# A mixer's attention weights for two of four head pairs turned by DMA transposes instead of TensorE, and its norms taken from row sums

## The chip, the cores and the metric

The kernel runs on one core of one Trainium2 chip. The core has a matrix engine (PE, with its own weight loads, PEld), a vector engine (DVE), a scalar engine (ACT), a further vector engine (POOL) and SP, which here issues DMAs. All engines run their own instruction streams in order and meet at semaphores. The metric is the device time of one execution in microseconds; lower is better.

## The reference

A decoder trunk of two layers over 256 tokens of width 1024. Each layer is a half FFN, a mixer and a second half FFN, each added to the scaled input and layer-normed:

```python
for l in range(DEPTH):                                          # 2
    h = _swiglu(x, ffn_w1[l, 0], ffn_w3[l, 0], ffn_w2[l, 0])    # 1024 -> 2816 -> 1024
    x = _layernorm(ALPHA * x + 0.5 * h, ln_g[l, 0], ln_b[l, 0])
    h = _mixer(x, l, ...)
    x = _layernorm(ALPHA * x + h, ln_g[l, 1], ln_b[l, 1])
    h = _swiglu(x, ffn_w1[l, 1], ffn_w3[l, 1], ffn_w2[l, 1])
    x = _layernorm(ALPHA * x + 0.5 * h, ln_g[l, 2], ln_b[l, 2])
```

The mixer projects x to u, v, q, k, val and two gates. Branch A is a gated unit with causal 128x128 position mixing. Branch B, which the change touches, is differential attention with 8 heads, each of two 64-wide query/key halves and a 128-wide value:

```python
p = jax.nn.softmax(where(mask, s, neg))     # s: b h m q k, m = 0, 1
a = p[:, :, 0] - lam * p[:, :, 1]           # the attention weights
o = einsum('bhqk,bkhe->bqhe', a, val)       # then a norm per head
```

The two branches, each times its gate, are summed and projected (w_out). Inputs and output are float32.

## The kernel before

**Tiles.** The 256 tokens are two tiles (t = 0, 1) of 128. Weights come from HBM in 1 MB chunks: `stream` issues one DMA on SP into `raw`, ACT copies each half to `whi` (line 174) and DVE subtracts to get the rest, `wlo` (line 178). A float32 product is three matmuls, hi·hi, lo·hi and hi·lo. `gemm_a2` does it with the weights as the stationary side: 16 matmuls `x,whi` 512 wide (line 283), then 16 `x,wlo` 256 wide (line 290), after which ACT takes one part of the bank out (`r`, line 291) and DVE adds the other (`gz` in the gates, line 293).

**Order.** PE runs in the order in which the program is written. The other engines' streams are ordered by a scheduler from priorities; `behind(x)` puts an instruction after x in that order, and `soon()` raises its priority. Side work is written as generators: `beside(task, d)` starts one after d beats of the main matmuls and `yield n` lets n beats pass, so that its PE instructions are put between the main ones. A beat is 0.65 for 8 matmuls of line 283 and 0.35 for 8 of line 290.

**A mixer.** The val gemm comes first, then eight `rope` gemms for q and k, two for each of four pairs of heads (hp = 0 to 3), then the gate gemms and the rest of branch A. `attend(hp)` runs as a side task: the scores of t=1 and then of t=0 on PE (line 837, into side banks), the masked maximum on DVE (845), Exp on ACT (847), `less` on DVE (856), which forms the weights a as `pp` tiles (128 queries by keys: 128x512 for t=1, 128x256 for t=0, two heads each). PE then turns them by six 128x128 transposes against an identity (871 and 876), ACT takes the two banks out to `aT` (873, 878), and PE multiplies them with val (884, 886). After that ACT copies the result out (`on`, 889) and squares it in its bank for the per-head norm (894, four times); POOL works out the reciprocal root; ACT scales (905), splits the halves of each float into two 16-bit planes (184), a DMA transpose on SP turns these (189), ACT joins the planes (195), and ACT and DVE form the operand `hb` (915, 916). So pair 2's work after its scores and pair 3's scores lie in the last q/k gemm and the first gate gemms; pair 3's transposes and value matmuls lie in the gate gemms.

**Banks and buffers.** PSUM has four main banks for the gemms and four side banks. Four 128x512 `pp` tiles belong to a pair's two score tiles (two halves each); `less` writes its result over one of the two and leaves the other unused.

**Norms.** After an FFN, `part_s` adds the product to x on DVE with the row sum as a by-product, and `finish_s` gets the mean from the sums, the variance from a Square on ACT with its own accumulation, and 1/sqrt by three steps on DVE. After a mixer, `part` adds and `bn_stats` (571) takes the statistics, `bn_aggr` (578) joins them, then the same three steps and the scaling (582). In both, the upper half of the normed tile goes out as 16-bit planes to a DMA transpose (`send`), the lower half is turned by PE (641), and ACT scales and splits both (646, 233, with DVE's 234) into the operand of the next FFN, whose first gemm starts with the parts of it that are there.

Of the kernel before, what the change touches and what calls it, by code (L numbers as in the profile page):

```python
# [15 lines left out]
U16 = mybir.dt.uint16  # L16
# [4 lines left out]
P = 128  # L21
# [37 lines left out]
def trunk(ctx, tc, x, xT, w13a, w13b, w2s, w2p, wb, wqk, wa, wbr, wo, gateb, sgug, sgub, sguwT, sgubias, lam, diffg,  # L59
# [25 lines left out]
    def side_bank():  # L85
        return psum.tile([P, 512], F32, tag="side", name=name("sbank"))
# [54 lines left out]
    def beside(task, delay):  # L141
        tasks.append([clock[0] + delay, task])
# [366 lines left out]
    class Norm:  # L509
# [29 lines left out]
            else:  # L539
                V.scalar_tensor_tensor(out=y, in0=y, scalar=scale, in1=v, op0=ALU.mult, op1=op)  # L540

        def part_s(self, t, c, ps):
            y = self.y[t][:, c * 512 : (c + 1) * 512]
            V.scalar_tensor_tensor(out=y, in0=y, scalar=1.0, in1=ps, op0=ALU.mult, op1=ALU.add,
                                   accum_out=self.st[t][:, c : c + 1])

        def finish_s(self, t, waits):
            y, st = self.y[t], self.st[t]
# [26 lines left out]
        def finish(self, t, waits):  # L575
            y = self.y[t]
            mv = sm("mv", 2)
            V.bn_aggr(out=mv, in_=self.st[t])
            if not self.last:
                r = rsqrt(mv[:, 1:2], self.eps)  # L580
                for s in (slice(512, D), slice(0, 512)):
                    self.ends[t] = V.tensor_scalar(out=y[:, s], in0=y[:, s], scalar1=mv[:, 0:1], scalar2=r,
                                                   op0=ALU.subtract, op1=ALU.mult).ins
                    if s.start:
                        self.send(t)
                beside(self.turned(t, waits), 0)
                return
            cuts = [slice(*c) for c in ((768, D), (0, 512), (512, 768))]
            ve, sd, r, a = (sm(n, 1) for n in ("ve", "nwy", "nwa", "nwy"))
            G.tensor_scalar(out=ve, in0=mv[:, 1:2], scalar1=self.eps, scalar2=None, op0=ALU.add)  # L590
            A.activation(sd, mv[:, 1:2], AF.Sqrt, bias=self.eps_t)
            rows = [y[:, s] for s in cuts]
            if t == NT - 1:
                rows[1:] = [side_bank()[:, : s.stop - s.start] for s in cuts[1:]]
                for b, s in zip(rows[1:], cuts[1:]):
                    PE.matmul(b, ident, y[:, s], start=True, stop=False)
                diag = self.minus[:, P : 2 * P]
                A.activation(diag, self.minus[:, :P], AF.Copy, scale=mv[:, 0:1])
                for b, s in zip(rows[1:], cuts[1:]):
                    PE.matmul(b, diag, self.g[:, s], start=False, stop=True)  # L600
            for s in cuts[: 1 if t == NT - 1 else 3]:
                V.scalar_tensor_tensor(out=y[:, s], in0=y[:, s], scalar=mv[:, 0:1], in1=self.g[:, s],
                                       op0=ALU.subtract, op1=ALU.mult)
            V.reciprocal(out=r, in_=sd)
            V.tensor_scalar(out=a, in0=r, scalar1=r, scalar2=ve, op0=ALU.mult, op1=ALU.mult)
            V.tensor_scalar(out=r, in0=a, scalar1=3.0, scalar2=r, op0=ALU.subtract, op1=ALU.mult)
            for n, (s, v) in enumerate(zip(cuts, rows)):
                V.scalar_tensor_tensor(out=y[:, s], in0=v, scalar=r, in1=self.b[:, s], op0=ALU.mult, op1=ALU.add)
                (nc.sync, A)[n % 2].dma_start(out[t * P : (t + 1) * P, s], y[:, s])
# [178 lines left out]
    def mixer(l, i, norm):  # L788
# [34 lines left out]
        def attend(hp, qT, kT):  # L823
# [27 lines left out]
            def less(t, pp):  # L851

                nk = (t + 1) * P
                for j in range(2):
                    s = slice(j * nk, (j + 1) * nk)
                    V.scalar_tensor_tensor(out=pp[0][:, s], in0=pp[1][:, s], scalar=c4[:, t * 2 + j : t * 2 + j + 1],
                                            in1=pp[0][:, s], op0=ALU.mult, op1=ALU.add)
                return pp[0]
# [3 lines left out]
            first = exps(0)  # L862
            V.reciprocal(out=rc, in_=sums[:, 4:])
            V.scalar_tensor_tensor(out=c4, in0=rc, scalar=neg_lam[l], in1=sums[:, :4], op0=ALU.mult, op1=ALU.mult)
            second, first = less(1, second), less(0, first)
            yield 2.6
            b = side_bank()
            for j in range(2):
                for c in range(2):
                    o = (j * 2 + c) * P  # L870
                    PE.transpose(b[:, o : o + P], second[:, o : o + P], ident)
            aT1 = slots("aT", 2)[0]
            A.activation(aT1, b, AF.Copy)
            b = side_bank()
            for j in range(2):
                PE.transpose(b[:, j * P : (j + 1) * P], first[:, j * P : (j + 1) * P], ident)
            aT0 = slots("aT", 2)[0][:, :T]
            A.activation(aT0, b[:, :T], AF.Copy)
            yield 2.3
            b = side_bank()  # L880
            for j in range(2):
                h = hp * 2 + j
# [120 lines left out]

        def done(t, ps):
            for h in range(2):
                ln.part(t, h * 512, ps[h])
            ln.finish(t, ((2, 1.5), (2, 1))[t])

        gemm_b2([wo[l, 0], wo[l, 1]], view(m_hi), view(m_lo), done)
        return ln.close()  # L1010
# [98 lines left out]
```

## Time and profile before

| | us |
|---|---|
| median of 3 runs | 1212.89 (1212.53 to 1213.18) |
| the profiled execution | 1213.48 |
| its span, first to last instruction | 1211.8 |
| PE busy | 1203.9 (99%) |
| DVE busy | 947.9 (78%) |
| ACT busy | 852.3 (70%) |
| POOL busy | 90.3 (7%) |

The span is what the profile's rows divide up; the 1.7 us between it and the execution's own time lies outside them. "Busy" is the time that at least one instruction of an engine was in flight. The granted clock of the matrix engine was 1.000 over the span. A row of the timeline gives the start, the duration, the engine, the line, the operation with its operands and the count of instructions that it joins; brackets hold the idle time before it and what ended that. Durations of rows that follow each other on DVE and ACT overlap by some 0.06 to 0.1 us, so steps are best read from start to start.

### The profile page before, as it was taken

To read this page: it belongs to the slowest core of one execution; us is meant where nothing else is said; L and a number is where in the kernel's file an instruction comes from. 1 tells how busy PE (TensorE), PEld (TensorE's weight loads), DVE (VectorE), ACT (ScalarE), POOL (GpSimd) and SP (SyncE) were. 2 spreads that over 40 slices of the span, in tenths; PEclk is the share of its full clock that TensorE was granted. 3 is DMA by queue.
4 is the path that set the end of the run, shared out by engine and by line. 5 is a ranking of instruction groups with operands and counts; after the bars stand their busy time and mean duration, and the time that the engine had idled before them with its cause. 6 is when DMAs were issued, how large, how long until landed. Compare 5 with 4: busy or idle time off the path is not lost.

```text
span 1211.8 us, 16532 instructions
## 1 busy us (share of the span) xinstructions
PE 1203.9 (99%) x5961; PEld 1011.5 (83%) x5961; DVE 947.9 (78%) x1540; ACT 852.3 (70%) x1376; POOL 90.3 (7%) x184
## 2 busy tenths in 40 slices
PE   9999999999999999999999999999999999999998
PEld 8888888888888878888888888888888888888886
DVE  6658998885696976579985679989756878847797
ACT  6677677679865585776776776776898555767761
POOL 0100000233300000000000000003331000000000
PEclk9999999999999999999999999999999999999999
DMA  8985665655764658666668665766648556676551
GB/s 321 317 267 174 212 249 204 231 178 164 229 227 168 217 180 280 191 187 218 232 210 274 194 179 209 252 226 197 211 143 273 176 174 217 203 257 210 184 204 46
DMA packets 101346, 257.00 MB, mean 212 GB/s; under 512 B 66528, under 2 KB 67600, under 8 KB 74640
## 3 DMA queue, kind: packets, MB, share of 16 engines
q1 hardware_dynamic: 97296, 243.03, 59.9%
q0 software_dynamic: 3536, 12.13, 3.2%
q8 instruction: 46, 0.75, 0.3%
q10 hardware_dynamic: 432, 0.79, 0.2%
q14 instruction: 36, 0.29, 0.1%
HBM read 235.47 MB, written 1.05 MB: 195 GB/s over the span
## 4 chain that ended last, share of the span: by engine, by line
PE 93%; DVE 5%; ACT 1%; issue 1%; DVEq 0%; ACTq 0%
PE bank L271 35%; PE sbank L271 24%; PE bank L283 17%; PE bank L290 9%; PE sbank L283 2%; PE bank L446 2%; PE sbank L290 1%; PE sbank L837 1%; PE sbank L969 1%; PE sbank L886 1%; DVE wlo L178 1%; DVE nwa L248 1%; DVE nwy L249 0%; DVE x L234 0%; DVE st L571 0%
## 5 line engine op out<-in xcount | busy, mean ns | idle before, releaser
L178 DVE TENSOR_TENSOR wlo<-raw,whi 128x1024 fp32r<-128x1024 f32 (+1 forms) x396 | 436.2, 1124 | 144.2 <-ACT whi L174 113.5
L174 ACT ACTIVATE whi<-raw 128x1024 fp32r<-128x1024 f32 (+1 forms) x396 | 372.9, 971 | 123.8 <-PE bank L283 40.1
L271 PE MATMUL bank<-whi,x 128*128 128x512 f32 x840 | 263.3, 390 | 0.0
L271 PEld LDWEIGHTS bank<-whi,x 128*128 128x128 f32 x840 | 157.7, 188 | 32.9
L271 PE MATMUL bank<-wlo,x 128*128 128x512 f32 x420 | 163.5, 389 | 0.0
L271 PE MATMUL sbank<-whi,x 128*128 128x512 f32 x512 | 158.9, 389 | 0.0
L283 PE MATMUL bank<-x,whi 128*128 128x512 f32 x640 | 156.0, 394 | 0.0
L283 PEld LDWEIGHTS bank<-x,whi 128*128 128x128 f32 x640 | 117.1, 188 | 26.4 <-issue 2.3
L271 PEld LDWEIGHTS sbank<-whi,x 128*128 128x128 f32 x512 | 96.1, 188 | 20.0
L353 ACT ACTIVATE shi<-raw 128x1024 fp32r<-128x1024 f32 (+1 forms) x80 | 73.4, 947 | 51.8 <-DVE raw L368 26.4
L271 PE MATMUL sbank<-wlo,x 128*128 128x512 f32 x256 | 99.6, 389 | 0.0
L355 DVE TENSOR_TENSOR slo<-raw,shi 128x1024 fp32r<-128x1024 f32 (+1 forms) x80 | 85.3, 1087 | 14.1 <-ACT shi L353 13.2
L271 PEld LDWEIGHTS bank<-wlo,x 128*128 128x128 f32 x420 | 78.9, 188 | 16.1
L290 PE MATMUL bank<-x,wlo 128*128 128x256 f32 x640 | 85.9, 285 | 0.0
L290 PEld LDWEIGHTS bank<-x,wlo 128*128 128x128 f32 x640 | 81.6, 191 | 2.2
L291 ACT ACTIVATE r<-bank 128x256 f32<-128x256 f32 x112 | 41.4, 376 | 24.0 <-PE bank L290 24.0
L271 PEld LDWEIGHTS sbank<-wlo,x 128*128 128x128 f32 x256 | 48.0, 188 | 9.9
L271 PE MATMUL sbank<-whi,hhi 128*128 128x512 f32 x144 | 56.3, 391 | 0.0
L271 PE MATMUL sbank<-whi,hlo 128*128 128x512 f32 x144 | 56.1, 389 | 0.0
L271 PE MATMUL sbank<-wlo,hhi 128*128 128x512 f32 x144 | 56.0, 389 | 0.0
L506 POOL DMA_DIRECT2D bc<-in_lng x6 | 3.2, 529 | 696.0 <-DVE bc L505 696.0
L710 ACT ACTIVATE planes<-silu 128x1024 uint16<-128x1024 uint16 x40 | 42.0, 1053 | 7.3 <-DVE silu L709 6.2
(249 smaller groups left out, 1997.7 us busy)
## 6 DMA issues: line engine op xcount, KB each, us to landing
raw<-in_w13b SPq DMA_DIRECT2D x76, 1024.0 KB, 5.3
raw<-in_w2p SPq DMA_DIRECT2D x24, 1024.0 KB, 4.9
raw<-in_wa SPq DMA_DIRECT2D x24, 1024.0 KB, 5.3
raw<-in_w2s SPq DMA_DIRECT2D x20, 1024.0 KB, 4.9
raw<-in_wb SPq DMA_DIRECT2D x16, 1024.0 KB, 5.1
raw<-in_wqk SPq DMA_DIRECT2D x16, 1024.0 KB, 4.9
raw<-in_wbr SPq DMA_DIRECT2D x16, 1024.0 KB, 4.8
raw<-in_w13a SPq DMA_DIRECT2D x8, 1024.0 KB, 4.8
```

The costliest lines, as they stand in the source:

```text
L174: copied = A.activation(h, r, AF.Copy)
L178: V.tensor_tensor(out=w, in0=r, in1=h.bitcast(F32), op=ALU.subtract)
L248: V.tensor_scalar(out=a, in0=y, scalar1=y, scalar2=ve, op0=ALU.mult, op1=ALU.mult)
L271: PE.matmul(ps, xx, w, start=start and n == 0, stop=stop and n == 2)
L283: PE.matmul(b[-1], hi[:, k * P : (k + 1) * P], xc(k), start=k == 0, stop=False)
L290: PE.matmul(b[n][:, :T], lo[:, k * P : (k + 1) * P], xc(k)[:, :T], start=False, stop=k == KT - 1)
L291: emptied[0] = A.activation(r[:, s], b[n][:, T:], AF.Copy, scale=scale).ins
L353: A.activation(h, r, AF.Copy)
L355: V.tensor_tensor(out=w, in0=r, in1=h.bitcast(F32), op=ALU.subtract)
L446: PE.matmul(ps[t][m], x[:, j, o + t * P : o + (t + 1) * P], y, start=k0 + j == 0 and o == 0 and y is hi, stop=k0 + j == KT - 1 and y is lo)
L710: A.activation(pk.rearrange("p (w k) -> p w k", w=2), s.bitcast(U16).rearrange("p (k w) -> p w k", w=2), AF.Copy)
L837: PE.matmul(banks[m][:, j * nk : (j + 1) * nk], rows(qT, m, j, t * P, P), rows(kT, m, j, 0, nk), start=True, stop=True)
```

## The change

1. In pairs 2 and 3 of each mixer, the six PE transposes and two ACT copies out of PSUM are replaced. DVE copies each weight tile into two 16-bit planes (new line 879), in the `pp` tile that `less` left unused; two DMA transposes on SP (8 and 4 blocks of 128x128 16-bit numbers) turn the planes; three beats later DVE joins the planes to `aT` and half a tile (new line 885), placed behind the latest add of a gemm's bank. The value matmuls follow two beats after that, where before they followed the transposes by 2.3.
2. The mixers' norms use `part_s` and `finish_s`. `bn_stats` and `bn_aggr` go, a Square on ACT comes; `part_s` gets the scale and the same `behind` that `part` had. Only the last norm still uses `finish`.

In a whole run that is 24 PE transposes, 8 ACT copies, 8 `bn_stats` and 4 `bn_aggr` fewer, and 16 DVE copies, 8 DMA transposes and 4 Squares with their small instructions more. The order of PE is otherwise the same, and POOL's too. Lines after the edit carry numbers shifted by -8 ahead of the new lines (837 is now 829) and by +8 behind them (894 is now 902).

```diff
--- before.py
+++ after.py
@@ -539,10 +539,11 @@
             else:
                 V.scalar_tensor_tensor(out=y, in0=y, scalar=scale, in1=v, op0=ALU.mult, op1=op)
 
-        def part_s(self, t, c, ps):
+        def part_s(self, t, c, ps, scale=1.0):
             y = self.y[t][:, c * 512 : (c + 1) * 512]
-            V.scalar_tensor_tensor(out=y, in0=y, scalar=1.0, in1=ps, op0=ALU.mult, op1=ALU.add,
-                                   accum_out=self.st[t][:, c : c + 1])
+            with behind(self.xlo.get((0, 0))):
+                V.scalar_tensor_tensor(out=y, in0=y, scalar=scale, in1=ps, op0=ALU.mult, op1=ALU.add,
+                                       accum_out=self.st[t][:, c : c + 1])
 
         def finish_s(self, t, waits):
             y, st = self.y[t], self.st[t]
@@ -576,15 +577,6 @@
             y = self.y[t]
             mv = sm("mv", 2)
             V.bn_aggr(out=mv, in_=self.st[t])
-            if not self.last:
-                r = rsqrt(mv[:, 1:2], self.eps)
-                for s in (slice(512, D), slice(0, 512)):
-                    self.ends[t] = V.tensor_scalar(out=y[:, s], in0=y[:, s], scalar1=mv[:, 0:1], scalar2=r,
-                                                   op0=ALU.subtract, op1=ALU.mult).ins
-                    if s.start:
-                        self.send(t)
-                beside(self.turned(t, waits), 0)
-                return
             cuts = [slice(*c) for c in ((768, D), (0, 512), (512, 768))]
             ve, sd, r, a = (sm(n, 1) for n in ("ve", "nwy", "nwa", "nwy"))
             G.tensor_scalar(out=ve, in0=mv[:, 1:2], scalar1=self.eps, scalar2=None, op0=ALU.add)
@@ -862,21 +854,37 @@
             first = exps(0)
             V.reciprocal(out=rc, in_=sums[:, 4:])
             V.scalar_tensor_tensor(out=c4, in0=rc, scalar=neg_lam[l], in1=sums[:, :4], op0=ALU.mult, op1=ALU.mult)
+            free2, free1 = second[1], first[1]
             second, first = less(1, second), less(0, first)
-            yield 2.6
-            b = side_bank()
-            for j in range(2):
-                for c in range(2):
-                    o = (j * 2 + c) * P
-                    PE.transpose(b[:, o : o + P], second[:, o : o + P], ident)
-            aT1 = slots("aT", 2)[0]
-            A.activation(aT1, b, AF.Copy)
-            b = side_bank()
-            for j in range(2):
-                PE.transpose(b[:, j * P : (j + 1) * P], first[:, j * P : (j + 1) * P], ident)
-            aT0 = slots("aT", 2)[0][:, :T]
-            A.activation(aT0, b[:, :T], AF.Copy)
-            yield 2.3
+            if hp < HEADS // 4:
+                yield 2.6
+                b = side_bank()
+                for j in range(2):
+                    for c in range(2):
+                        o = (j * 2 + c) * P
+                        PE.transpose(b[:, o : o + P], second[:, o : o + P], ident)
+                aT1 = slots("aT", 2)[0]
+                A.activation(aT1, b, AF.Copy)
+                b = side_bank()
+                for j in range(2):
+                    PE.transpose(b[:, j * P : (j + 1) * P], first[:, j * P : (j + 1) * P], ident)
+                aT0 = slots("aT", 2)[0][:, :T]
+                A.activation(aT0, b[:, :T], AF.Copy)
+                yield 2.3
+            else:
+                half = slots("half", 2)[0]
+                tts = []
+                for (p, spare), dst in (((second, free2), slots("tt", 2)[0]), ((first, free1), half[:, :T])):
+                    pk = spare.bitcast(U16)
+                    V.tensor_copy(pk.rearrange("p (w k) -> p w k", w=2), p.bitcast(U16).rearrange("p (k w) -> p w k", w=2))
+                    tts.append(turning(pk, pk.shape[1] // (2 * P), dst))
+                yield 3
+                aT1, aT0 = slots("aT", 2)[0], half[:, T:]
+                for dst, tt in zip((aT1, aT0), tts):
+                    with behind(added[0]):
+                        V.tensor_copy(dst.bitcast(U16).rearrange("p (k w) -> p k w", w=2),
+                                      tt.rearrange("p (w k) -> p k w", w=2))
+                yield 2
             b = side_bank()
             for j in range(2):
                 h = hp * 2 + j
@@ -1003,8 +1011,8 @@
 
         def done(t, ps):
             for h in range(2):
-                ln.part(t, h * 512, ps[h])
-            ln.finish(t, ((2, 1.5), (2, 1))[t])
+                ln.part_s(t, h, ps[h], ln.scale)
+            ln.finish_s(t, ((2, 1.5), (2, 1))[t])
 
         gemm_b2([wo[l, 0], wo[l, 1]], view(m_hi), view(m_lo), done)
         return ln.close()
```

Three places show what moves on DVE and ACT. All are in the mixer of layer 0.

First DVE, between `less` of pair 2 (856) and the scores of pair 3: `qk` is pair 3's k operand, `gz` the first gate tiles. Before:

```order
L856 SCALAR_TENSOR_TENSOR pp_2583<-pp_2588,c_2528,pp_2583 128x128 x2
L817 TENSOR_TENSOR qk_2547<-qk_2547,swap_2546 128x512
L178 TENSOR_TENSOR wlo_2966<-raw_2959,whi_2965 128x1024
L293 TENSOR_TENSOR gz_2610<-bank_2568,r_2609 128x256
L293 TENSOR_TENSOR gz_2610<-bank_2599,r_2609 128x256
L178 TENSOR_TENSOR wlo_3038<-raw_3035,whi_3037 128x1024
L178 TENSOR_TENSOR wlo_3042<-raw_3035,whi_3041 128x1024
L293 TENSOR_TENSOR gz_2698<-bank_2667,r_2697 128x256
L293 TENSOR_TENSOR gz_2698<-bank_2676,r_2697 128x256
```

and with the change:

```order
L879 COPY pp_2541<-pp_2536 128x1024
L879 COPY pp_2588<-pp_2583 128x512
L809 TENSOR_TENSOR qk_2547<-qk_2547,swap_2546 128x512
L178 TENSOR_TENSOR wlo_2960<-raw_2953,whi_2959 128x1024
L293 TENSOR_TENSOR gz_2616<-bank_2568,r_2615 128x256
L293 TENSOR_TENSOR gz_2616<-bank_2605,r_2615 128x256
L178 TENSOR_TENSOR wlo_3032<-raw_3029,whi_3031 128x1024
L178 TENSOR_TENSOR wlo_3036<-raw_3029,whi_3035 128x1024
L293 TENSOR_TENSOR gz_2692<-bank_2673,r_2691 128x256
L885 COPY aT_2726<-tt_2600 128x1024
L885 COPY half_2599<-half_2599 128x512
L293 TENSOR_TENSOR gz_2692<-bank_2682,r_2691 128x256
```

The two plane copies stand ahead of the `qk` add on which the next scores depend, and the two joins ahead of the second add of the second `gz`.

Second ACT, from pair 1's `on` (889, with the four squares of its bank) to the second gate tile. Before:

```order
L889 ACTIVATE on_2636<-sbank_2629 128x512
L894 ACTIVATE sbank_2629,ss_2638<-sbank_2629 128x128
L174 ACTIVATE whi_3037<-raw_3035 128x1024
L894 ACTIVATE sbank_2629,ss_2638<-sbank_2629 128x128
L932 ACTIVATE gate_2554<-gz_2610,gbh 128x256
L894 ACTIVATE sbank_2629,ss_2638<-sbank_2629 128x128
L932 ACTIVATE gate_2554<-gz_2610,gbh 128x256
L894 ACTIVATE sbank_2629,ss_2638<-sbank_2629 128x128
L873 ACTIVATE aT_2690<-sbank_2685 128x512
L878 ACTIVATE aT_2695<-sbank_2692 128x256
L174 ACTIVATE whi_3041<-raw_3035 128x1024
L291 ACTIVATE r_2697<-bank_2667 128x256
```

and with the change:

```order
L174 ACTIVATE whi_3031<-raw_3029 128x1024
L897 ACTIVATE on_2642<-sbank_2635 128x512
L940 ACTIVATE gate_2554<-gz_2616,gbh 128x256
L902 ACTIVATE sbank_2635,ss_2644<-sbank_2635 128x128
L940 ACTIVATE gate_2554<-gz_2616,gbh 128x256
L902 ACTIVATE sbank_2635,ss_2644<-sbank_2635 128x128
L174 ACTIVATE whi_3035<-raw_3029 128x1024
L902 ACTIVATE sbank_2635,ss_2644<-sbank_2635 128x128
L291 ACTIVATE r_2691<-bank_2673 128x256
L902 ACTIVATE sbank_2635,ss_2644<-sbank_2635 128x128
L291 ACTIVATE r_2691<-bank_2682 128x256
L940 ACTIVATE gate_2555<-gz_2692,gbh 128x256 x2
```

The two `aT` copies are gone; the last two squares of line 894 (now 902) stand behind a weight copy and a bank's `r` copy.

Third DVE again, at the joins of pair 3; `turned` and `hb` are pair 0's. Before:

```order
L916 SCALAR_TENSOR_TENSOR hb_1906<-turned_2881,dgs,hb_1906 128x256
L916 SCALAR_TENSOR_TENSOR hb_1907<-turned_2881,dgs,hb_1907 128x256
L293 TENSOR_TENSOR gz_2909<-bank_2872,r_2908 128x256
L293 TENSOR_TENSOR gz_2909<-bank_2887,r_2908 128x256
L178 TENSOR_TENSOR wlo_3179<-raw_3176,whi_3178 128x1024
```

and with the change:

```order
L293 TENSOR_TENSOR gz_2818<-bank_2808,r_2817 128x256
L924 SCALAR_TENSOR_TENSOR hb_1906<-turned_2884,dgs,hb_1906 128x256
L924 SCALAR_TENSOR_TENSOR hb_1907<-turned_2884,dgs,hb_1907 128x256
L293 TENSOR_TENSOR gz_2900<-bank_2875,r_2899 128x256
L885 COPY aT_2934<-tt_2803 128x1024
L885 COPY half_2802<-half_2802 128x512
L293 TENSOR_TENSOR gz_2900<-bank_2890,r_2899 128x256
```

The two joins stand behind the two `hb` rows and the first `gz` add.

## The prediction

> **What bounds the kernel now.** I read the page first: busy times, then the chain that ended last.
>
> ```profile
> PE 1203.9 (99%) x5961; PEld 1011.5 (83%) x5961; DVE 947.9 (78%) x1540; ACT 852.3 (70%) x1376; POOL 90.3 (7%) x184
> PE 93%; DVE 5%; ACT 1%; issue 1%; DVEq 0%; ACTq 0%
> ```
>
> PE has work in flight 99% of the span, and the chain runs over PE for 93% of it. So an edit pays only by what it takes out of PE's stream, and costs only where it makes PE wait. The view of PE's waits says how little it waits today: its largest items beyond the start and the end are at the mixers' norms.
>
> ```profile
> PE sbank L641 <- DVE xtok L582: 0.9, 2, 0.5
> ```
>
> Then I read the timeline of the two stretches that the change touches, in layer 0 (layer 1 repeats them 599 us later), engine by engine. All times below are us from the span's start.
>
> **What the attention part takes off PE.** The six transposes of a pair stand in one place of PE's stream:
>
> ```profile
> 285.62 0.60 PE L871 MATMUL sbank<-ident,pp 128*128 128x128 f32 x4
> 286.20 2.15 PE L290 MATMUL bank<-x,wlo 128*128 128x256 f32 x16
> 288.18 3.82 PE L283 MATMUL bank<-x,whi 128*128 128x512 f32 x16
> 298.74 2.08 PE L290 MATMUL bank<-x,wlo 128*128 128x256 f32 x16
> 300.65 1.55 PE L283 MATMUL bank<-x,whi 128*128 128x512 f32 x6
> ```
>
> From the first transpose to the next matmul are 286.20 - 285.62 = 0.58. The 16 matmuls behind take 288.18 - 286.20 = 1.98, the same 16 with nothing ahead 300.65 - 298.74 = 1.91, so another 0.07. A site is worth 0.65, and the four sites (two pairs, two layers) **2.6 us**, or 0.21%. That is the whole possible gain of this part; the eight ACT copies that go lie off PE's path.
>
> One rule speaks against the move. The Trainium skill, "VectorE: DVE Perf Modes", Rules for kernel authors, says to turn a 128x128 block on TensorE if PSUM will do as destination, and gives 390 ns there against 1309 ns by DMA. By that figure 8 blocks one after another would be an estimated 10.5 us and would come after their use. The DMA transposes of 8 blocks that the kernel already makes (`tt<-both`) are the nearer evidence:
>
> ```profile
> L189 SPq DMA_TRANSPOSE tt<-both x8: 1238/1253/1320, 269.1 to 912.5; - x8
> DMA to landing us min/median/max: 2.7/2.7/8.1
> ```
>
> All 8 blocks land 2.7 after the issue (median), an issue holds SP for 1.25, and one in the trace took 8.1.
>
> **What it puts on DVE.** The trace has no such copy; its price is bounded by these rows:
>
> ```profile
> 417.14 0.15 DVE L241 TENSOR_SCALAR ve<-mv 128x1 f32<-128x1 f32 x1
> 419.19 1.00 DVE L582 TENSOR_SCALAR xtok<-xtok,mv,nwy 128x512 f32<-128x512 f32 x2
> 267.98 1.40 DVE L856 SCALAR_TENSOR_TENSOR pp<-pp,c,pp 128x256 f32<-128x256 f32 x4
> 269.30 0.68 DVE L817 TENSOR_TENSOR qk<-qk,swap 128x512 f32<-128x512 f32 x1
> 269.90 1.22 DVE L178 TENSOR_TENSOR wlo<-raw,whi 128x1024 fp32r<-128x1024 f32 x1
> ```
>
> With one source in SBUF, 512 elements twice take 1.00 (line 582); with two sources 512 take 0.68 (817) and 1024 take 1.22 (178). From 512 to 1024 elements two-source work grows by 0.54, so a one-source copy at twice that rate is 0.15 + 0.53 = 0.68 for 1024 and 0.15 + 0.27 = 0.42 for 512 (the low bound; line 582, at 0.5 each with two steps in one instruction, lies a little above it). The high bound is the two-source rate, 1.22 and 0.68. I take the low one, as line 582 is the nearest row. DVE rows overlap their followers by 0.08, so the two copies take 0.60 + 0.33 = 0.93 of DVE's time, and the two joins the same.
>
> The same page ("What auto-detection actually checks") gives two elements a cycle to a one-source operation in SBUF whose outermost dimensions are even, as these are, and four only with unit steps, which every second 16-bit number is not. Line 582 agrees with the two; no run so far shows the copy.
>
> **Pair 2, layer 0: where the delay goes.** DVE's weight remainders in this stretch are made long ahead: the one that starts at 269.90 (wlo_2966 in the order rows) is read by the matmuls of line 290 behind pair 3's value matmuls, which start at 292.79, 23 us later. So late ones cost nothing here. What counts is the chain through `gz`, ACT and the scores:
>
> ```profile
> 271.04 0.75 DVE L293 TENSOR_TENSOR gz<-bank,r 128x256 f32<-128x256 f32 x2
> 271.49 0.51 ACT L932 ACTIVATE gate<-gz,gbh 128x256 f32<-128x256 f32 x1
> 271.90 0.26 ACT L894 ACTIVATE sbank<-sbank 128x128 f32<-128x128 f32 x1
> 273.60 1.05 ACT L174 ACTIVATE whi<-raw 128x1024 fp32r<-128x1024 f32 x1
> 277.09 0.50 ACT L847 ACTIVATE pp<-pp,mx 128x256 f32<-128x256 f32 x1
> ```
>
> The plane copies start when `less` ends, at 269.38 + 0.04, where the `qk` add started at 269.30: +0.12 + 0.93 = +1.05. The scores that need `qk` are due at 272.55 - 0.65 = 271.90, the add ends at 270.35 + 0.68: hidden. The `gz` add and with it ACT's gate go from 271.49 to 272.54. ACT's new order from there, start to start, is gate 0.41, square 0.28, gate 0.40, square 0.28, weight 0.95, square 0.28, `r` 0.26, so the last square starts at 275.40 and ends at 275.66. The weight copy ends at 274.96, its remainder takes DVE to 276.14, `gz` to 276.48; then the two joins. The transposes' issues stand at 270.31 (behind pair 1's, at 269.06 for 1.25) and 271.56, and land by 274.3: 2.2 or more to spare. The two issues hold SP for 2.5 ahead of the next weight chunk's, which the 23 us cover. The joins end at 277.49. The second `gz` starts at 277.41, ACT's gate 0.45 behind it as at 271.49, and the exponentials 0.41 later, at 278.28 instead of 277.09 (**+1.19**).
>
> On PE:
>
> ```profile
> 257.27 1.13 PE L837 MATMUL sbank<-qk,qk 64*128 64x256 f32 x8
> 258.33 1.90 PE L283 MATMUL bank<-x,whi 128*128 128x512 f32 x7
> 272.55 1.59 PE L837 MATMUL sbank<-qk,qk 64*128 64x256 f32 x8
> 274.07 2.11 PE L283 MATMUL bank<-x,whi 128*128 128x512 f32 x8
> 276.11 0.71 PE L837 MATMUL sbank<-qk,qk 64*128 64x128 f32 x8
> 279.67 0.39 PE L884 MATMUL sbank<-val,aT 128*128 128x128 f32 x2
> ```
>
> The scores of t=1 take 1.06 for pair 2 (257.27 to 258.33) and 1.52 for pair 3: 0.46 of waiting inside, for the bank that the squares of line 894 still hold. With two side banks fewer in use, the scores of t=0 get that bank: due at 276.11 - 0.65 - 0.46 = 275.00, free at 275.66, so 0.66 of waiting in place of 0.46. Pair 2's value matmuls are due at 279.67 - 0.65 - 0.46 + 0.66 = 279.22; the half tile is there at 277.49. No wait.
>
> **Pair 3, layer 0.** The chain is ACT's row up to `r`, then DVE:
>
> ```profile
> 289.52 0.59 ACT L873 ACTIVATE aT<-sbank 128x512 f32<-128x512 f32 x1
> 290.26 0.65 ACT L291 ACTIVATE r<-bank 128x256 f32<-128x256 f32 x2
> 289.67 0.48 DVE L916 SCALAR_TENSOR_TENSOR hb<-turned,dgs,hb 128x256 fp32r<-128x256 f32 x1 [0.20 <-ACT hb L915]
> 283.37 1.40 DVE L856 SCALAR_TENSOR_TENSOR pp<-pp,c,pp 128x256 f32<-128x256 f32 x4
> 292.79 0.39 PE L884 MATMUL sbank<-val,aT 128*128 128x128 f32 x2
> ```
>
> ACT has hardly any idle time from the exponentials on, so I carry the +1.19. The two `aT` copies, 290.26 - 289.52 = 0.74, are gone: `r` at 290.71, its first half done at 291.07. DVE's second `hb` row starts at 290.86, `gz` at 291.26, the joins at 291.60 and 292.20; they end at 292.61. With 0.25 for semaphore and weight load the value matmuls start at 292.86. They are due at 292.79 - 0.65 - 0.46 + 0.66 - 0.65 = 291.69, so PE **waits 1.17**, and layer 0 ends at +0.07: the gain is eaten. The transposes are in time: `less` ends by 284.77 + 1.19, the copies by 286.9, the second issue stands at 287.9 at the latest and lands at 290.6.
>
> **Layer 1.** DVE's row comes 599.00 later (868.30 against 269.30); PE's, counted from where it would stand without the 0.46 of waiting, 875.52 - 275.65 = 599.87 later:
>
> ```profile
> 868.30 0.68 DVE L817 TENSOR_TENSOR qk<-qk,swap 128x512 f32<-128x512 f32 x1
> 875.52 0.72 PE L837 MATMUL sbank<-qk,qk 64*128 64x128 f32 x8
> 892.19 0.39 PE L884 MATMUL sbank<-val,aT 128*128 128x128 f32 x2
> ```
>
> The bank is free at 874.66 and wanted at 875.52 - 0.65 = 874.87: no wait. The value matmuls of pair 3 start at 292.86 + 599.00 = 891.86 instead of 892.19: -0.33. **Attention in all: +0.07 - 0.33 = -0.26.**
>
> **The norms.** From the first tile's add to the start of 1/sqrt:
>
> ```profile
> 415.44 0.69 DVE L568 SCALAR_TENSOR_TENSOR xtok<-xtok,bank 128x512 f32<-128x512 f32 x1 [0.22 <-PE bank L271]
> 171.76 0.69 DVE L544 SCALAR_TENSOR_TENSOR xtok<-xtok,sbank 128x512 f32<-128x512 f32 x1
> 174.02 0.15 DVE L243 TENSOR_SCALAR ve<-ss 128x1 f32<-128x1 f32 x1 [1.31 <-ACT sq L552]
> 430.78 0.14 DVE L241 TENSOR_SCALAR ve<-mv 128x1 f32<-128x1 f32 x1
> 433.51 0.39 PE L271 MATMUL bank<-whi,x 128*128 128x512 f32 x1
> 434.35 0.66 PE L641 MATMUL sbank<-ident,xtok 128*128 128x128 f32 x4 [0.45 <-DVE xtok L582]
> ```
>
> By bn_stats 417.14 - 415.44 = 1.70; by sums and the Square after an FFN 174.02 - 171.76 = 2.26. For the first tile the 0.56 is largely given back, since one weight copy less stands ahead of its scaling on ACT; I charge 0.1. For the second tile the Square stands behind a split on ACT (`ve` at about 430.4 for 430.78), but two weight remainders of 0.55 each then precede the steps on DVE: +0.2 on line 641's wait (433.51 + 0.23 to 434.35, 0.61 today). Two layers, with the parts rounded up: **+0.4**. Bounds: both 0.61 waits vanish (-1.2), or the whole 0.56 counts at both tiles (+2.2); I take +0.4 because DVE, not ACT, is full there.
>
> **Sum.** -0.26 + 0.4 = +0.14, on the profiled execution's 1213.48 (span 1211.8 and 1.7 around it) 1213.6. That execution stands 0.59 above the median of the runs, so the median should be **1213.0**. This kernel's runs spread by 0.05%, and what can be told from no change is about 0.2%, or 2.4 us: I forecast no change.
>
> **The rivals.**
> *Faster.* The chain to the joins is added up from start-to-start times over 20 us on two engines; if it comes out 1.2 shorter at pair 3, PE waits for nothing there, and the change gives -2.6, less the 0.46 of the old bank wait, plus 0.4: 1210.2. For it: ACT loses 8 copies, and both engines have idle time before pair 2. Against it: DVE gains 1.86 a pair in a row where ACT waits for it. 0.27.
> *Slower: copies at the two-source rate.* Then each couple of copies costs 0.54 + 0.26 = 0.8 more: at pair 2's copies, its joins and pair 3's joins, 2.4 on the chain, all of it waiting on PE at pair 3 as the slack there is used up: +2.5 and +2.1 in the layers, +0.4 from the norms, 1217.9. It decides from 0.3 per copy on. For it: 16-bit elements two apart, and POOL reading SBUF alongside. Against it: line 582. 0.17.
> *Slower: transposes late.* With 8.1 to landing instead of 2.7, pair 2's joins are 3 late and DVE's whole row behind them: +2.6 a layer past the slack, about 1218. For it: at least one of eight did so. Against it: no chunk of weights is being issued right ahead. 0.06.
> *The norms the other way,* -1.2 instead of +0.4: 1211.4, still no change. 0.05.
> That leaves 0.45 for the forecast. Faster by over 0.2% (below 1210.5): 0.27 and 0.03 of the forecast's edge, 0.30; slower (above 1215.3): 0.23 and 0.02, 0.25; the same 0.45. The forecast's own range is 1211.5 to 1214.8; the range given reaches to the faster case and most of the slower, 1209.9 to 1217.4.
>
> **What would show it.** The copies at 0.68 and 0.42 (or 1.22 and 0.68); the new transposes landing in 2.7; PE without line 871 in pairs 2 and 3, and a wait of 1.2 before pair 3's value matmuls in layer 0, of 1.0 in layer 1, with none at pair 2; 0.7 inside the t=0 scores of layer 0; line 641's wait at 0.8. No wait at pair 3 makes the forecast wrong towards faster; a wait at pair 2's value matmuls towards slower.

## The result and the profile after

| | before | the change |
|---|---|---|
| median, us (6 runs each) | 1212.84 (1212.53 to 1213.26) | 1217.73 (1217.07 to 1218.5) |
| ratio, with its 95% interval | | 1.0040 (1.0029 to 1.0051) |
| the profiled execution, us | 1213.48 | 1217.62 |
| its span, us | 1211.8 | 1215.9 |

The change costs 4.9 us. The forecast was 1213.0, no change, with a range that ended at 1217.4. PE's busy time fell from 1203.9 to 1202.2 us, so the loss is waiting. Ratios leave out three single executions of the later sets that took 1920, 2255 and 5096 us. The page's chain that ended last, and the largest items of the view of PE's waits, for the kernel with the change:

```profile
PE 86%; ACT 6%; DVE 4%; POOL 2%; issue 1%; DMA 0%; DVEq 0%; ACTq 0%
```

```profile
PE bank L271 <- DVE gz L293: 3.4, 2, 1.7
PE sbank L892 <- DVE half L885: 1.3, 2, 0.6
...
PE sbank L633 <- DVE xtok L556: 0.7, 2, 0.4
...
PE sbank L829 <- ACT sbank L902: 0.5, 1, 0.5
PE bank L283 <- DVE gz L293: 0.3, 2, 0.2
```

PE's share of the chain fell from 93% to 86%, and ACT, which had 1%, has 6%. The columns of the second are the total in us, the count and the longest. Its second, third and fourth rows are the ones that the prediction had: before pair 3's value matmuls, at the norms, inside the scores. The first, 1.7 us in each layer, it did not have, nor the last, at a bank inside the gate gemms. The first is twice in PE's timeline, once in each layer, at the first matmuls behind the gate gemms. The same place of layer 0, first before, then with the change (the sixth matmul of line 271, which starts a new bank):

```profile
311.78 0.40 PE L271 MATMUL bank<-whi,x 128*128 128x512 f32 x1
...
312.94 0.63 PE L271 MATMUL bank<-whi,x 128*128 128x512 f32 x2
```

```profile
311.58 0.40 PE L271 MATMUL bank<-whi,x 128*128 128x512 f32 x1
...
312.74 0.39 PE L271 MATMUL bank<-whi,x 128*128 128x512 f32 x1
314.79 0.50 PE L271 MATMUL bank<-whi,x 128*128 128x512 f32 x1 [1.66 <-DVE gz L293]
```

Before, the sixth matmul is the second of the row at 312.94 and starts at 312.94 + 0.23 = 313.17. With the change it starts at 314.79.

**Where the wait comes from.** The bank is one whose sum DVE adds (`gz`, line 293) after ACT has copied the other part out (`r`, line 291). ACT runs in order, and between the two `r` copies of this gate tile stands its scaling of pair 3 (`both`), which needs POOL's reciprocal root. Back from there the chain goes over POOL, pair 3's squares and `on`, ACT's scaling of pair 2, POOL again, and pair 2's squares to the exponentials of pair 3. Its links in the timelines of POOL, ACT and DVE, before:

```profile
277.09 0.50 ACT L847 ACTIVATE pp<-pp,mx 128x256 f32<-128x256 f32 x1
289.31 0.22 POOL L897 TENSOR_TENSOR ss<-s,ss 128x4 f32<-128x4 f32 x1 [11.05 <-ACT sbank L894]
296.40 1.28 ACT L905 ACTIVATE both<-on,nwy 128x128 f32<-128x128 f32 x4 [0.63 <-POOL nwy L264]
297.71 1.06 ACT L184 ACTIVATE both<-both 128x1024 uint16<-128x1024 uint16 x1
298.94 0.59 ACT L889 ACTIVATE on<-sbank 128x512 f32<-128x512 f32 x1
303.00 0.22 POOL L897 TENSOR_TENSOR ss<-s,ss 128x4 f32<-128x4 f32 x1 [6.63 <-ACT sbank L894]
310.99 1.28 ACT L905 ACTIVATE both<-on,nwy 128x128 f32<-128x128 f32 x4 [2.27 <-POOL nwy L264]
312.57 0.43 DVE L293 TENSOR_TENSOR gz<-bank,r 128x256 f32<-128x256 f32 x1 [2.26 <-ACT r L291]
```

and with the change:

```profile
277.63 0.49 ACT L839 ACTIVATE pp<-pp,mx 128x256 f32<-128x256 f32 x1
289.85 0.21 POOL L905 TENSOR_TENSOR ss<-s,ss 128x4 f32<-128x4 f32 x1 [9.78 <-ACT sbank L902]
297.23 1.28 ACT L913 ACTIVATE both<-on,nwy 128x128 f32<-128x128 f32 x4 [2.62 <-POOL nwy L264]
298.42 1.04 ACT L174 ACTIVATE whi<-raw 128x1024 fp32r<-128x1024 f32 x1
299.37 1.04 ACT L184 ACTIVATE both<-both 128x1024 uint16<-128x1024 uint16 x1
300.58 0.58 ACT L897 ACTIVATE on<-sbank 128x512 f32<-128x512 f32 x1
304.63 0.22 POOL L905 TENSOR_TENSOR ss<-s,ss 128x4 f32<-128x4 f32 x1 [7.43 <-ACT sbank L902]
312.73 1.28 ACT L913 ACTIVATE both<-on,nwy 128x128 f32<-128x128 f32 x4 [2.38 <-POOL nwy L264]
314.31 0.43 DVE L293 TENSOR_TENSOR gz<-bank,r 128x256 f32<-128x256 f32 x1 [2.26 <-ACT r L291]
```

The two executions differ by 0.82 us ahead of this stretch, 0.80 of it within their first 8 us (the 16 matmuls of line 283 ahead of pair 2's transposes start at 266.24 before and at 265.42 now), so 0.82 is added to a time of the changed kernel to compare it:

| link | later by, us |
|---|---|
| exponentials of pair 3 | 277.63 + 0.82 - 277.09 = 1.36 |
| POOL's root of pair 2 starts | 1.36 |
| ACT scales pair 2 | 1.65 |
| `on` of pair 3 | 2.46 |
| POOL's root of pair 3 starts | 2.45 |
| ACT scales pair 3 | 2.56 |
| `gz`, which frees the bank | 2.56 |
| PE's sixth matmul | 314.79 + 0.82 - 313.17 = 2.44 |

The copies and joins at pair 2 bring 1.36, which the prediction put at 1.19. POOL's slower work in between brings 0.29, the weight copy that now stands between pair 2's scaling and its planes (298.42) another 0.81, the last links 0.10. Of the 2.56 only 0.12 was free: before, `gz` ended at 313.00 and the matmul started at 313.17. The rest is in the layer's time, whatever PE had saved on the way. PE does not lose all of the 2.44 there. It is 0.15 behind after pair 3's value matmuls (294.41 + 0.82 - 295.08) and 0.62 at the end of the gate gemms (311.58 + 0.82 - 311.78), as a bank that the `gz` at 305.39 frees, from the same late row of ACT, comes late too (the last row of the waits above). The wait at the sixth matmul adds 1.82. In layer 1 the changed kernel's PE is 867.53 - 866.07 = 1.46 behind at the 16 matmuls ahead of pair 2's place, and 916.55 - 912.57 = 3.98 behind at the matmul behind the wait: 2.52. There it is 0.21 behind after the value matmuls and 0.66 at the end of the gate gemms. The two layers make 4.96, the medians 4.9; the two profiled executions are only 4.14 apart, since the changed one starts with the 0.82 in hand.

### The profile page after: what moved, and what is told of

The parts are those of the page before. It is cut to its first block, busy times and chain, and to the rows that moved or that the text cites. A ratio compares the mean times of both kernels' runs of the same rounds, so it can differ in the third digit from the quotient of the medians.

```text
span 1215.9 us, 16536 instructions
## 1 busy us (share of the span) xinstructions
PE 1202.2 (99%) x5937; PEld 1008.4 (83%) x5937; DVE 949.7 (78%) x1556; ACT 854.4 (70%) x1376; POOL 90.1 (7%) x184
## 4 chain that ended last, share of the span: by engine, by line
PE 86%; ACT 6%; DVE 4%; POOL 2%; issue 1%; DMA 0%; DVEq 0%; ACTq 0%
PE bank L271 35%; PE sbank L271 24%; PE bank L283 13%; PE bank L290 7%; PE sbank L283 2%; PE bank L446 2%; PE sbank L290 1%; ACT whi L174 1%; PE sbank L829 1%; ACT both L913 1%; PE sbank L977 1%; POOL nwa L262 1%; POOL nwa L263 1%; POOL nwy L264 1%; ACT pp L839 1%
```

## The experiments

The theory, called the chain theory below: a layer's time here is set by that chain, which starts with VectorE's added work at pair 2 and ends at a bank that PE wants at the end of the gate gemms. What PE saves ahead of that point is waited away. The rival: pair 3's value matmuls come late, since their joins are late, and the rest follows from them. The kernels were timed in three sets, each beside the kernel before, whose medians there were 1213.32 (for the first four kernels below), 1212.87 (for the first try with VectorE's work, the two versions of the change with ACT's order and the value matmuls moved, and the control of the kernel before) and 1212.57 (for the rest); each difference is against its own set, from 4 to 10 executions.

**The attention part alone.** Part 1 of the change, with the mixers' norms as before (the branch of `finish` that the change took out is back too, not shown here):

```diff
-                ln.part_s(t, h, ps[h], ln.scale)
-            ln.finish_s(t, ((2, 1.5), (2, 1))[t])
+                ln.part(t, h * 512, ps[h])
+            ln.finish(t, ((2, 1.5), (2, 1))[t])
```

> The attention part of the change alone; the mixers' norms stay with bn_stats. Chain theory (the time of a layer is set by a chain on ACT, POOL and ACT that starts at pair 2's copies and joins on DVE and ends 40 us later at a bank that PE wants when the gate gemms are over): as slow as the whole change, +4.9 us (+4.4 to +5.4), with PE waiting 1.7 for gz there in each layer. If the norms had a share, the difference to the whole change is their share; I expect under 0.4 us either way.

Measured: 1217.73, +4.4, ratio 1.0039 (1.0024 to 1.0054), beside 1.0040 for the whole change. The wait for `gz` is in its waits with the same 3.4, and at the norms it keeps the 0.9 of the kernel before. The norm part costs and gains nothing that shows.

**One pair at a time.** Only pair 2, or only pair 3, by DMA transposes:

```diff
-            if hp < HEADS // 4:
+            if hp != 2:
                 yield 2.6
```

and `hp != 3` in the other kernel.

> Only pair 2 is turned by DMA transposes, pair 3 stays with TensorE (norms as in the change). Chain theory: the delay enters at pair 2, so the loss stays nearly whole, +4 to +5 us, although PE does six transposes more per layer than with the whole change. Rival (pair 3's late joins and value matmuls are what makes the rest late): no loss, -1.3 us from two sites of 0.65, to 0.

Measured: 1219.34, +6.0, ratio 1.0051 (1.0036 to 1.0066).

> Only pair 3 is turned by DMA transposes (norms as in the change). Chain theory with nothing but DVE's delay at pair 2 as cause: no loss and no gain, -0.5 to +0.5, as PE waits for the chain whatever it saves. Chain theory with ACT's own order counted: here two weight copies (0.95 each) stand between pair 2's planes and pair 3's copy of its result, so the chain is 1.9 later per layer: +3 to +3.8 us. Rival (pair 3's joins and late value matmuls): +3.5 to +5.

Measured: 1215.78, +2.5, ratio 1.0022 (1.0013 to 1.0032). The waits of PE, first with only pair 2, then with only pair 3:

```profile
PE bank L271 <- DVE gz L293: 3.4, 2, 1.7
PE sbank L977 <- DVE vg L959: 1.5, 1, 1.5
PE sbank L829 <- ACT sbank L902: 1.1, 2, 0.6
```

```profile
PE bank L283 <- DVE gz L293: 2.7, 2, 1.4
...
PE sbank L892 <- DVE half L885: 0.3, 2, 0.2
```

With pair 2 alone there is no late value matmul and the loss is larger than the whole change's; the rival had this kernel at a gain. That it is more than the forecast 4 to 5 goes with one more wait, 1.5 in layer 1, before the spatial matmuls (line 977), and with 1.1 in place of 0.5 inside the scores. With pair 3 alone there is a loss too, where VectorE's delay at pair 2 alone as a cause would have none; the version of the theory that counts ACT's order, with two weight copies behind pair 2's planes, had the sign and a little more than the size. The rival's +3.5 to +5 overlaps this run's interval (+1.6 to +3.9 us), but PE waits only 0.3 for the joins here and 2.7 for `gz`. The wait sits one gate tile earlier than I had it (line 283).

**ACT's scaling of pair 3 behind the copy that frees the bank.**

```diff
             r = rsqrt4(ss, 1.0 / (2 * HD))
-            yield 2
+            yield 2.35 if hp == 3 else 2
```

> The whole change, but ACT's scaling of pair 3 (line 913) waits 2.35 beats instead of 2 after POOL's work is issued, which puts it behind the copy r that frees the bank PE waits for. Chain theory: PE's waits of 1.7 for gz vanish in both layers, and what stays is what PE lost earlier: 1213.5 to 1214.3 us, -3.5 to -4.2 against the whole change. Rival (late value matmuls): the wait only changes its place, +4 to +5 us against the kernel before.

Measured: 1216.83, +3.5, ratio 1.0030 (1.0018 to 1.0042). The chain theory's number missed; the rival's lies inside the interval (+2.2 to +5.1 us), and a wait did change its place. The wait at the bank is gone, as the chain theory had it, but a new one stands before the spatial matmuls, 1.6 in the two layers. PE's timeline in layer 0:

```profile
349.49 0.94 PE L977 MATMUL sbank<-wsT,vg 128*128 128x128 f32 x6 [0.77 <-DVE vg L959]
```

ACT's row is still late by what it was: its order has changed at one place only. After pair 3 it goes on to the last `hb` and the u/v branch, whose norm on DVE feeds the spatial matmuls; PE waited 0.2 for it in the kernel before too. So the chain has a next end 36 us further on with as little room as the first.

**VectorE's added work without the rest, first try.** The kernel before, with pair 2's plane copies and joins added and their results unused; TensorE turns both pairs.

```diff
+            free2, free1 = second[1], first[1]
             second, first = less(1, second), less(0, first)
+            idle = hp == 2
+            if idle:
+                for p, spare in ((second, free2), (first, free1)):
+                    V.tensor_copy(spare.bitcast(U16).rearrange("p (w k) -> p w k", w=2), p.bitcast(U16).rearrange("p (k w) -> p w k", w=2))
             yield 2.6
...
-            yield 2.3
+            yield 0.4
+            if idle:
+                for p, spare in ((second, free2), (first, free1)):
+                    with behind(added[0]):
+                        V.tensor_copy(p.bitcast(U16).rearrange("p (k w) -> p k w", w=2), spare.bitcast(U16).rearrange("p (w k) -> p k w", w=2))
+            yield 1.9
```

> The kernel before, with the four VectorE copies of pair 2 added and their results unused; TensorE still turns both pairs, nothing is late for the value matmuls. Chain theory: the delay alone makes the loss: exponentials of pair 3 about 2 us later (1.05 for the plane copies, 0.94 for the joins), carried over ACT and POOL to the bank at the end of the gate gemms, +2 to +3.5 per layer, +4 to +7 us in all. Rival (the loss comes from the DMA transposes' lateness at pair 3, or from TensorE's freed time): within 0.5 us of the kernel before.

Measured: 1215.51, +2.6, ratio 1.0023 (1.0013 to 1.0032): neither theory's number. This edit did more than it meant to. Splitting the pause put the value matmuls of all four pairs eight matmuls later, and ACT's order came out with both `r` copies of the gate tile ahead of pair 3's scaling, so the link to the bank was cut. There is a loss without any DMA transpose, but this run does not say which of its changes makes it.

**The same, with the orders kept.** The copies back are a task of their own, so PE's order is that of the kernel before, and ACT's order has pair 3's scaling between the two `r` copies and a weight copy behind pair 2's scaling, both as in the change.

```diff
+            free2, free1 = second[1], first[1]
             second, first = less(1, second), less(0, first)
+            if hp == 2:
...
+                def back():
+                    for p, spare in ((second, free2), (first, free1)):
+                        with behind(added[0]):
+                            V.tensor_copy(p.bitcast(U16).rearrange("p (k w) -> p k w", w=2), spare.bitcast(U16).rearrange("p (w k) -> p k w", w=2))
+                    yield 0
+
+                beside(back(), 3)
             yield 2.6
```

> The kernel before with pair 2's four VectorE copies added and their results unused, this time with PE's order exactly as before and ACT's order with pair 3's scaling (905 in the kernel before) between the two copies r of one gate tile, as in the change. Chain theory: about 2 us of VectorE work ahead of pair 3's exponentials, plus a weight copy that stands behind pair 2's scaling as in the change, reach PE as a wait for gz at the end of the gate gemms: +2.0 to +2.9 a layer, +4 to +6 us, as much as the change loses, although nothing of its DMA transposes or of its late value matmuls is there. Rival (those are the cause): within 0.7 us of the kernel before.

Measured: 1217.35, +4.8, ratio 1.0038 (1.0023 to 1.0053). PE's timeline in layer 0, where the wait is:

```profile
313.35 0.39 PE L271 MATMUL bank<-whi,x 128*128 128x512 f32 x1
315.44 0.50 PE L271 MATMUL bank<-whi,x 128*128 128x512 f32 x1 [1.71 <-DVE gz L293]
```

No DMA transpose, no late value matmul, none of TensorE's work saved, and yet the whole loss of the change, with the same 3.4 us of waiting, over both layers, at the same matmul. The time follows the chain and not PE's work. The run holds VectorE's delay and ACT's weight copy together. Its timeline of layer 0, compared with the kernel before like the table above (0.61 between the two executions), has pair 3's exponentials late by 2.07, pair 2's scaling by 2.08, `on` of pair 3, behind the weight copy, by 2.88 and `gz` by 3.00.

**ACT's order changed for both pairs.** The whole change, with a longer pause before the scaling of pairs 2 and 3; ACT then copies and squares pair 3's result before it stops for POOL's root of pair 2.

```diff
             r = rsqrt4(ss, 1.0 / (2 * HD))
-            yield 2
+            yield 3 if hp >= 2 else 2
```

> The whole change, with ACT's scaling (line 913) of pairs 2 and 3 issued 3 beats instead of 2 after POOL's work. That puts pair 3's result copy and squares ahead of pair 2's scaling on ACT, so ACT no longer stands still for POOL ahead of them. Chain theory: the waits for gz at the end of the gate gemms and the wait before the spatial matmuls both go; what stays is PE's wait before pair 3's value matmuls, 0.8 to 0.9 per layer, and inside the scores: +0.3 to +1.2 us against the kernel before. Rival (late value matmuls at the root): +3 us or more.

Measured: 1212.61, -0.3, ratio 0.9998 (0.9989 to 1.0007), a little under the forecast. ACT's timeline with this edit, at the place of the table above:

```profile
295.15 0.60 ACT L897 ACTIVATE on<-sbank 128x512 f32<-128x512 f32 x1
...
299.83 1.27 ACT L913 ACTIVATE both<-on,nwy 128x128 f32<-128x128 f32 x4
```

`on` of pair 3 moved from 300.58 to 295.15, and the scaling behind it finds POOL's root done. Both waits, for `gz` and before the spatial matmuls, are gone from PE's waits. What is left of those in the change is the one before pair 3's value matmuls:

```profile
PE sbank L892 <- DVE half L885: 1.3, 2, 0.6
```

**And pair 3's value matmuls eight matmuls later.** The edit also gives pair 2's scaling a fourth beat.

```diff
                                       tt.rearrange("p (w k) -> p k w", w=2))
-                yield 2
+                yield 2.35 if hp == 3 else 2
...
             r = rsqrt4(ss, 1.0 / (2 * HD))
-            yield 2
+            yield {2: 4, 3: 3}.get(hp, 2)
```

> As the run before this one, and pair 3's value matmuls come 0.35 beats (8 matmuls of line 290, 0.95 us) later. Then the joins are in time. Chain theory: 1.5 to 2 us less than the run before this one, so -0.5 to -1.5 us against the kernel before: the first version in which the time taken off PE shows in the total. If the later value matmuls put the chain on ACT back, the waits for gz return and it is over +1.

Measured: 1210.98, -1.9, ratio 0.9987 (0.9977 to 0.9996), a little more than forecast. The wait before pair 3's value matmuls is gone from PE's waits; what pair 2's fourth beat does by itself was not tried.

> The same version once more beside the others, for its interval and as their base: 0.998 to 0.999 of the kernel before, -1.4 to -2.4 us.

Measured: 1210.97, -1.6, ratio 0.9986 (0.9976 to 0.9996). This version is faster than both kernels: by 1.6 to 1.9 us than the kernel before (the intervals reach from 0.5 to 2.9), by 6.5 to 6.8 than the change as it was.

**Controls.** The kernel before with 3 beats ahead of the scaling (the diff is against it), and the faster version with `part` and `finish` in the mixers' norms as in the first experiment:

```diff
             r = rsqrt4(ss, 1.0 / (2 * HD))
-            yield 2
+            yield 3 if hp >= 2 else 2
```

> Control: the kernel before with the same 3 beats in place of 2 for pairs 2 and 3 and nothing else. PE waits for nothing there in the kernel before, so no gain is to be had beyond the 0.2 before the spatial matmuls of layer 0: -0.5 to +0.3 us.

Measured: 1213.33, +0.5, ratio 1.0002 (0.9992 to 1.0011): nothing. This new order of ACT has no gain of its own; it lets the time taken off PE count.

> The version with ACT's scaling and pair 3's value matmuls later, with the mixers' norms by bn_stats as in the kernel before: what the norm part is worth where PE is waited for. PE's wait at the norms' transposes was 0.9 in all with bn_stats and 0.7 to 0.8 with row sums, so within 0.4 us of that version; -1.5 to -2.2 against the kernel before.

Measured: 1210.96, -1.6, ratio 0.9986 (0.9976 to 0.9996): the norms make no difference here either.

**Three pairs.** The faster version with pair 1 turned by DMA transposes too (`if hp < 1` for the transposes on TensorE).

> The version with ACT's scaling and pair 3's value matmuls later, and pair 1 turned by DMA transposes too. If PE is what bounds now, two more sites of 0.65 show: -1.3 us against that version, -3 us against the kernel before. If VectorE's two further couples of copies (1.9) set a chain late ahead of pair 2, up to +3 us against that version.

Measured: 1222.07, +9.5, ratio 1.0077 (1.0062 to 1.0092), far outside what was expected. PE's waits:

```profile
PE sbank L829 <- ACT sbank L902: 5.2, 2, 2.6
PE sbank L829 <- DVE qk L809: 4.3, 2, 2.6
```

Pair 3's scores wait 2.6 for the rotated k operand in layer 0 and 1.7 in layer 1, and 2.6 for their bank in each. On DVE the `qk` add of that operand waits for POOL's half of the rotation:

```profile
272.74 0.69 DVE L809 TENSOR_TENSOR qk<-qk,swap 128x512 f32<-128x512 f32 x1 [3.08 <-POOL swap L805]
```

The traces show where POOL's lateness begins, though no run tests it. On SP pair 1's two DMA transposes (252.85 and 254.28) stand ahead of the DMAs that feed the rotation of pair 3's q, which start at 257.07 and in the faster version at 252.88. POOL's half of that rotation starts at 263.75 instead of 257.41, POOL's root of pair 0 comes behind it, and the half for k behind that, at 271.44 instead of 264.58. The waits are not the whole price either: behind them, in layer 0, the granted clock is 0.50 from 280 to 284 us, and 8 matmuls of line 283 take 3.58 (280.81 to 284.39); in layer 1, at a clock of 1.00, they take 1.95.

## Why the prediction was wrong

- **The work taken off PE, 0.65 a site.** Right as far as it shows: in PE's timeline pair 3's site is shorter by just that (284.70 to 286.61 for 285.62 to 288.18), and with the waits out of the way 1.6 to 1.9 us of the 2.6 are in the total.
- **The price of the copies, 0.68 and 0.42.** Right to the hundredth: the joins take 0.68 and 0.42, as DVE's timeline of the changed kernel has them, the plane copies 0.69 and 0.41 at the extremes. The rival at the two-source rate falls.
- **The transposes in time.** Right: median 2.7 us to landing, and no wait for one in the attention weights.

```profile
275.83 0.68 DVE L885 COPY aT<-tt 128x1024 uint16<-128x1024 uint16 x1
276.43 0.42 DVE L885 COPY half<-half 128x512 uint16<-128x512 uint16 x1
```

- **Pair 2's chain, +1.19 at the exponentials; 0.66 inside the scores; no wait at pair 2's value matmuls.** Right but for a size: 1.36, and no wait at the value matmuls. Inside the scores of t=0 the profile has 0.52 idle, but from start to start they take 1.64 (274.20 to 275.84) for 0.65 without a wait, so 0.99 is lost and not 0.66.
- **Pair 3's wait, 1.17 and 1.0 against value matmuls due without it; layer 0 at +0.07 there.** Too high: the profile has 0.64 and 0.65 idle, and by the starts the matmuls wait 0.80 (292.01 - 290.26 for 0.95 before) and 0.81. In layer 0 they start at 292.01 + 0.82 - 292.79 = +0.04, where the sum had +0.07; the place is right, as the joins set it, and PE had lost 0.33 more in the scores and so waited less here. The 0.25 that the sum puts between joins and matmuls has no row behind it; it is 0.05 (291.54 + 0.42 to 292.01):

```profile
292.01 0.49 PE L892 MATMUL sbank<-val,half 128*128 128x128 f32 x2 [0.64 <-DVE half L885]
```

- **"So PE waits 1.17, and layer 0 ends at +0.07".** This is the step that failed. The chain was carried 20 us over ACT and DVE up to pair 3's joins, and dropped there, as if nothing but the value matmuls hung on it. ACT's row itself, late by the same 1.36, goes on: over POOL's root of pair 2, pair 3's squares and POOL's root of pair 3 to the copy that frees a bank, where 0.12 was free. At that bank it adds some 1.8 to each layer, 3.7 in all, and at the bank of line 283 ahead of it 0.5 to each: 4.6 of the 4.96 us. The term was put at nothing, and it was not among the rivals either. ACT's new order, a weight copy on that chain, was not priced: 0.81 of the 2.56. The rows for it were in the trace of before: ACT's scaling idle for POOL by 2.27 at 310.99, `gz` idle for ACT by 2.26 and ending at 313.00, the matmul at 313.17. Only PE's waits were read, and PE did not wait there yet.
- **Layer 1, -0.33 by more room.** Wrong: its waits are those of layer 0, 0.6 at the value matmuls and 1.7 at the bank. Inside its scores, where none was forecast, 0.62 is lost (876.32 to 877.59 for 0.65), and the value matmuls start at 893.76 - 1.46 - 892.19 = +0.11.
- **The norms, +0.4.** Too high: the faster version takes the same with and without them, to 0.01 us, in one set (the change itself, in two sets, has ratios of 1.0040 and 1.0039), and line 641's wait (now 633) fell from 0.9 to 0.7. From the second tile's first add to its scaling DVE takes 6.11 (428.48 to 434.59), for 6.18 before (427.12 to 433.30). The forecast's parts, 0.1 and 0.2 in each of two layers, make 0.6 and not 0.4.
- **The slower rival's 1217.9** meets the measured time by its number alone. Its mechanism, copies at half the rate, did not happen.

## What to carry to other kernels

A delay on an engine that runs in order doesn't end at its first consumer: follow the engine's own row on until it stands idle by more than the delay for something that is not late itself, through the engines that it feeds, and look at each place where a busy engine takes a buffer back with little room, even if it waits for nothing there yet. Where an instruction that waits for a slow third engine stands between two copies that free buffers, work saved ahead of it is lost; moving that instruction behind the copies is what lets the saving count. Here pair 2's instruction had to move as well; with pair 3's moved alone a wait stood further on. Before the size of a theory is tested by adding its cause alone, see that the orders of the other engines stay as they were: the first try here changed PE's order and cut the link on ACT that it was to test, the second kept PE's order and had ACT's as the change has it.

## What was not expected of the hardware

POOL's tiny steps, four elements for each partition, take 0.20 us alone, and about 1.1 while VectorE runs its weight remainders, which read two tensors in SBUF. With the change, POOL's and DVE's timelines:

```profile
292.12 0.20 POOL L264 TENSOR_TENSOR nwy<-nwa,yi 128x4 f32<-128x4 f32 x1
292.40 1.08 POOL L261 TENSOR_TENSOR nwa<-nwy 128x4 f32<-128x4 f32 x1
293.56 1.06 POOL L262 TENSOR_TENSOR nwa<-nwa,ve 128x4 f32<-128x4 f32 x1
...
292.21 3.48 DVE L178 TENSOR_TENSOR wlo<-raw,whi 128x1024 fp32r<-128x1024 f32 x3
```

A POOL step that starts during one of VectorE's remainders (1.22 each) ends about when that does, so POOL's roots of pairs 2 and 3 last 7.4 and 8.1 us (289.85 to 297.20 and 304.63 to 312.69), where pair 1's, beside fewer remainders, lasts 4.8 (275.23 to 280.07). The Trainium skill's "GPSIMD Engine Reference" says in its Specifications that POOL shares its SBUF interfaces with VectorE and contends with instructions that have two SBUF inputs; these rows agree. One of the change's joins, which read one tensor, does it too: the step at 291.10 takes 0.58 and ends at 291.68, the join at 290.94 + 0.69 = 291.63. In this chain POOL's two roots, in ACT's way, are the longest links, and where VectorE's work falls among their steps decides tenths of a microsecond.
